# A decoder layer on one core: its first stage in a written order, and the inputs of later blocks staged ahead

## The chip, the core and the metric

The kernel runs on one core of a Trainium2 chip, written in Tile, a layer over the engines' instructions that places buffers, semaphores and the order of work. TensorE (PE; its weight loads are shown as PEld) multiplies matrices into PSUM banks, VectorE (DVE), ScalarE (ACT) and GpSimd (POOL) do elementwise work, SyncE (SP) issues most of the DMAs. The metric is the device time of one execution in microseconds.

## The reference, cut to what matters

One layer of a decoder over 2048 tokens of width 1024, all in float32:

```python
mod = jax.nn.silu(c) @ w_ada[l] + b_ada[l]
shift_a, scale_a, gate_a, shift_m, scale_m, gate_m = [
    m[:, None, :] for m in jnp.split(mod, N_MOD, axis=-1)]
h = rms_norm(x, g_attn[l]) * (1.0 + scale_a) + shift_a
proj = h @ w_in[l]
q_f, k_f, v_f, q_s, k_s, v_s, f_logit = jnp.split(proj, offsets, axis=-1)
o_fox = forgetting_attention(...)      # 8 heads, causal
o_sb = stick_breaking_attention(...)   # 8 heads, causal
x = x + gate_a * (mix @ w_out[l])
h = rms_norm(x, g_mlp[l]) * (1.0 + scale_m) + shift_m
u = causal_depthwise_conv(h @ w_up[l], conv_w[l], conv_b[l])
x = x + gate_m * ((jax.nn.silu(u_gate) * u_val) @ w_down[l])
return rms_norm(x, g_final)
```

The first work is the condition: `silu(c) @ w_ada` for the first two of six parts (shift and scale of the mixer), a vector of 2048 numbers from a matrix of 8.4 MB. No query, key or value can be computed before it.

## The kernel before, in words

**Precision.** A float32 matrix is split into a high half, rounded to the type that TensorE takes, and the remainder. `split` (L43) writes the high half with ScalarE (L44) and the remainder, the low half, with GpSimd or, where it is given, VectorE (L45). A product is three matmuls: high by high, high by low, low by high (`accumulate`, L323).

**Blocks and units.** The tokens are four blocks of 512 (`TB`). A unit is one kind of head, one pair of heads and one block. Units run in the order stick-breaking pairs 0 to 3, then forgetting pairs 0 to 3, each over its four blocks. The first four units (pair 0, "direct") are special: their blocks must first be read from x, normalized, transposed and modulated to h. h is then stored in DRAM (`hs`), and the other pairs read it back (`proj`, L446). The first block is `first_block` (L458), the next three are `norm_proj` (L495).

**The first stage.** c is transposed to a column and put through SiLU. `begin_block` (L180) loads the x of a block as four tiles of 128 x 1024 and normalizes them: a sum of squares on ScalarE (L95), its root (L96), a reciprocal and a scaling on VectorE (L104). `load_ada` (L190) loads w_ada in four groups, and `load_raw` (L209) the first pair's weights between them. `first_block` transposes x on PE and copies it to a stage in SBUF, by ScalarE and VectorE in turn. For each second of the eight 128-row tiles `mod_cols` (L253) makes four columns of shift and scale: ScalarE scales three of eight terms by the condition's column (L256), GpSimd adds them (L258), VectorE multiplies and adds the other five (L261), and PE sums over the partitions by a product with ones (L264). Then ScalarE applies scale and shift (L476), the result is split, and PE adds it to the query and the key sums. `finish_proj` (L350) evicts both in halves (L355, L356 for the query), copies them by DMA into the layouts that attention reads (L360, L375), and makes the values (L396), 24 matmuls for each 128 tokens.

**Differences of values.** Stick-breaking attention uses each value less the one before it. `steps_of_values` (L432) stores the values to DRAM (`vd`), reads them back one row later and subtracts on GpSimd (L441).

**Blocks 1 to 3.** `norm_proj` calls `modulate` (L106): for each tile four transposes into PSUM, scale and shift on VectorE (L114), a split, the store of h and the query product. Then comes `begin_block` of the next block, and `finish_proj`.

**What sets the order.** Attention is a generator of steps, and so are the projections. `interleave` and `pace` (L760) let a count of projection steps pass for each attention step; `proj_steps` (L731) says how many steps a unit has. What is written so is only a priority. At the end Tile simulates all instructions and issues on each engine, whenever it is free in that simulation, the earliest one in the program whose inputs and buffers are ready. Each engine, and SyncE's DMA queue, then runs its list strictly in that order on the chip. `tc.issue_after(ins)` adds the rule that what is traced in its block comes behind `ins` on `ins`'s engine. The kernel before uses it for the stores of the first block's h, three behind the key copies and five behind the fetch of the values (L487 to L493).

**Buffers that matter.** `xt` has four tiles of x; tags K and V have five tiles each, one for each block's keys and values and one to spare; `pt` has three PSUM banks, `pj` and `qk` two each.

## Time and profile before

| | |
|---|---|
| median of three runs | 3090.65 us (3089.12 to 3095.47) |
| profiled execution | 3093.19 us |
| its span, first to last instruction | 3091.5 us |
| mean granted TensorE clock | 0.986 |
| instructions in the profile | 45281 |

The profile is of one execution. A row of a group gives the line, the engine, the operation, the tiles it writes and reads, shapes, count, then the time it was busy in all, the mean of one in ns, and the idle time of the engine just before with what ended it. A row of the timeline gives start, length, engine, and in brackets the idle time before it. A row of the chain of waits gives start, length and what the chain that ended last did then. A granted clock of 0.50 means that TensorE ran at half speed.

### The profile page before, as it was taken

What the parts mean: (1) busy time and instruction counts of PE and PEld (TensorE: products, weight loads), DVE (VectorE), ACT (ScalarE), POOL (GpSimd) and SP (SyncE); (2) the same over time, 40 slices, a digit from 0 to 9 for tenths busy, and PEclk for the clock granted to TensorE, in tenths of its full rate; (3) what the DMA queues carried; (4) which work ended last, traced back from release to release, by engine and by line L of the source; (5) the groups of instructions that cost most, each with busy time, mean ns of one, the idle gap of its engine ahead of it and who ended that gap; (6) DMA issues with size and microseconds to landing.
All of it is one profiled execution on the core that took longest, in us unless ns stands there. A gap on an engine that the chain in (4) does not pass through costs nothing.

```text
span 3091.5 us, 45281 instructions
## 1 busy us (share of the span) xinstructions
PE 2944.7 (95%) x15902; PEld 2501.1 (81%) x15902; DVE 2079.9 (67%) x3174; ACT 1680.7 (54%) x3121; POOL 986.4 (32%) x1015
## 2 busy tenths in 40 slices
PE   6899999999999999999999899999899998999998
PEld 5788889888888898888877688888688887888887
DVE  5778778877876567578633677778977776254253
ACT  5667767777775656568643544444444444343332
POOL 4431222142122322321122344444444442332321
PEclk9999999999999999999999999999999999999999
DMA  7748756766479755856166522222322224555562
GB/s 236 264 139 305 235 192 204 285 230 216 166 239 348 248 186 183 295 196 222 59 214 224 183 82 85 85 83 80 92 75 82 82 82 158 179 198 170 180 204 86
DMA packets 302676, 546.79 MB, mean 177 GB/s; under 512 B 30992, under 2 KB 179216, under 8 KB 301424
## 3 DMA queue, kind: packets, MB, share of 16 engines
q1 hardware_dynamic: 289712, 531.24, 52.5%
q10 hardware_dynamic: 12736, 12.66, 1.2%
q8 instruction: 125, 2.05, 0.3%
q14 instruction: 103, 0.84, 0.1%
HBM read 407.14 MB, written 130.36 MB: 174 GB/s over the span
## 4 chain that ended last, share of the span: by engine, by line
PE 54%; DMA 13%; DVE 12%; POOL 8%; issue 8%; ACT 4%; SPq 1%; POOLq 0%; ACTq 0%; DVEq 0%
PE ps_pj L325 9%; PE ps_o L1155 8%; PE ps_pv L531 7%; PE ps_pt L522 6%; PE ps_pj L396 4%; PE ps_t L1155 4%; PE ps_o L1005 4%; PE ps_bc L1155 4%; DMA wuraw<-in_w_up_dram 3%; PE ps_qk L512 3%; PE ps_qk L513 3%; DVE wu L45 3%; DMA r<-rstd 2%; DVE u L1074 2%; POOL ws L993 2%
## 5 line engine op out<-in xcount | busy, mean ns | idle before, releaser
L1005 PE MATMUL ps_o<-oa,wu 128*128 128x512 f32 x2088 | 503.1, 392 | 14.5 <-DVE oa L45 7.0
L1005 PEld LDWEIGHTS ps_o<-oa,wu 128*128 128x128 f32 x2088 | 390.0, 188 | 106.0 <-DVE oa L45 11.6
L325 PE MATMUL ps_pj<-hp,w_qk 128*128 128x512 f32 x1512 | 420.7, 406 | 23.0 <-DMA hp<-hs 12.9
L527 DVE TENSOR_TENSOR at<-ps_pt,at 128x512 fp32r<-128x512 f32 (+1 forms) x576 | 366.3, 652 | 103.2 <-ACT at L526 100.0
L531 PE MATMUL ps_pv<-at,V 128*128 128x256 f32 x2304 | 407.8, 294 | 19.3 <-ACT at L526 7.6
L550 DVE TENSOR_TENSOR_SCAN a<-r,a 128x512 f32<-128x512 f32 (+2 forms) x320 | 370.1, 1175 | 79.4 <-ACT a L545 38.9
L526 ACT ACTIVATE at<-ps_pt 128x512 fp32r<-128x512 f32 (+1 forms) x576 | 318.7, 576 | 152.3 <-PE ps_pt L522 113.8
L531 PEld LDWEIGHTS ps_pv<-at,V 128*128 128x128 f32 x2304 | 336.3, 191 | 56.0 <-DVE at L527 19.7
L325 PEld LDWEIGHTS ps_pj<-hp,w_qk 128*128 128x128 f32 x1512 | 275.0, 192 | 78.3 <-DMA hp<-hs 15.0
L45 DVE TENSOR_TENSOR wd<-wdraw,wd 128x1024 fp32r<-128x1024 f32 x88 | 113.3, 1288 | 261.2 <-ACT wd L44 261.0
L512 PE MATMUL ps_qk<-K,Q 128*128 128x512 f32 (+2 forms) x640 | 264.8, 415 | 5.7 <-DVE mn L588 2.6
L1155 PE MATMUL ps_o<-wd,g 128*128 128x512 f32 x1040 | 250.4, 390 | 8.7 <-ACT g L44 8.7
L45 POOL TENSOR_TENSOR g<-graw,g 128x512 fp32r<-128x512 f32 x84 | 141.8, 1690 | 325.9 <-ACT g L44 316.8
L1005 PE MATMUL ps_t<-ob,wu 128*128 128x512 f32 x984 | 243.2, 392 | 0.0
L396 PE MATMUL ps_pj<-w_v,hp 128*128 128x256 f32 (+1 forms) x1536 | 237.4, 289 | 2.4 <-DVE q L356 1.0
L1155 PEld LDWEIGHTS ps_o<-wd,g 128*128 128x128 f32 x1040 | 195.9, 189 | 49.9 <-ACT g L44 9.2
L513 PE MATMUL ps_qk<-K,Q 128*128 128x512 f32 (+2 forms) x640 | 236.3, 370 | 0.0
L44 ACT ACTIVATE wu<-wuraw 128x512 fp32r<-128x512 f32 x214 | 133.2, 626 | 187.6 <-PE ps_o L1005 118.4
L396 PEld LDWEIGHTS ps_pj<-w_v,hp 128*128 128x128 f32 x1536 | 210.9, 190 | 13.4 <-DVE q L356 2.2
L1005 PEld LDWEIGHTS ps_t<-ob,wu 128*128 128x128 f32 x984 | 186.3, 189 | 39.1 <-ACT hf_m L910 0.2
L44 ACT ACTIVATE wd<-wdraw 128x1024 fp32r<-128x1024 f32 x88 | 93.0, 1057 | 212.6 <-PE ps_bc L1155 200.6
L544 ACT ACTIVATE r<-ps_qk 128x512 f32<-128x512 f32 (+2 forms) x320 | 173.2, 541 | 52.0 <-PE ps_qk L513 49.9
(226 smaller groups left out, 5480.6 us busy)
## 6 DMA issues: line engine op xcount, KB each, us to landing
hp<-hs SPq DMA_DIRECT2D x224, 512.0 KB
wuraw<-in_w_up_dram SPq DMA_DIRECT2D x84, 512.0 KB
wdraw<-in_w_down_dram SPq DMA_DIRECT2D x84, 512.0 KB
g<-u SPq DMA_DIRECT2D x42, 512.0 KB
graw<-g SPq DMA_DIRECT2D x84, 256.0 KB
hs<-hp SPq DMA_DIRECT2D x32, 512.0 KB
hp<-in_w_ada_dram SPq DMA_DIRECT2D x32, 512.0 KB
qk_fox<-q SPq DMA_DIRECT2D x32, 512.0 KB
```

What stands on the lines that cost most here:

```text
L44: nc.scalar.activation(hi, src, AF.Copy)
L45: (lo_engine or nc.gpsimd).tensor_sub(lo, src, f(hi))
L325: nc.tensor.matmul(acc, w[kt][:, a, n], h[:, bb], start=kt == 0 and i == 0, stop=kt == KT - 1 and i == 2)
L396: nc.tensor.matmul(av[:, t * width:(t + 1) * width], hts[kt][:, a, tok], w[1][kt][:, bb, 0:width], start=kt == 0 and m == 0, stop=kt == KT ...
L512: nc.tensor.matmul(b[:, :cw], Q[:, hl, 0, qcols], K[:, hl, :cw], start=True, stop=False)
L513: marks.append(nc.tensor.matmul(b[:, :cw], Q[:, hl, 1, qcols], K[:, hl, :cw], start=False, stop=True).ins)
L526: nc.scalar.activation(at[:, 0, lo:], b[:, lo:], AF.Copy)
L527: nc.vector.tensor_sub(at[:, 1, lo:], b[:, lo:], f(at[:, 0, lo:]))
L531: nc.tensor.matmul(o[:, 0:2 * P], V[kt // 4][:, kt % 4, hl, :], rhs, start=first and kk == 0 and w == 0, stop=last and kk == 1 and w == 1)
L550: nc.vector.tensor_tensor_scan(rev, r[:, 0:need][:, ::-1], rev, 0.0 if right[qi] is None else right[qi][:, 0:1], ALU.mult, ALU.add)
L1005: nc.tensor.matmul(b, w[:, p, j], o[:, q], start=first and i == 0, stop=last and i == 2, skip_group_check=True)
L1155: nc.tensor.matmul(banks[t][n], g[:, a, t * P:(t + 1) * P], w[:, b, n * TB:(n + 1) * TB], start=k == 0 and i == 0, stop=k == NKD - 1 and i ...
```

## The change

The first stage is written in a fixed order: every part is traced inside `fixed()`, which puts its instructions behind the last one so traced on each engine. The small loads move from ScalarE's queue to SyncE's, between and behind the large ones. The eight terms of a column are six on VectorE (the first a scaling), and two that go straight to PE as products with the condition's column (a constant moving operand); a reduction on VectorE adds the three sums. All stage copies are on ScalarE. The low halves of the first pair's weights and of h are on VectorE. Small products without a use (`keep_warm`) run before and between. The first block's h is stored tile by tile as it is made. x of block 1 is loaded in the first stage, normalized after the first pair's value weights, and transposed and modulated into free K buffers between the first four steps of `finish_proj` and its rest. Blocks 2 and 3 are staged in free K and V buffers as the first eight steps of their projection; then x of the next block is loaded, then come eight steps of split and product, then the normalization of the next block, then `finish_proj`. Scale and shift of staged tiles alternate between ScalarE and VectorE.

```diff
+    @contextmanager
+    def fixed():
+        with ExitStack() as order:
+            for ins in last.values():
+                order.enter_context(tc.issue_after(ins))
+            n = len(nc.cur_bb.bb.instructions)
+            yield
+        for ins in nc.cur_bb.bb.instructions[n:]:
+            last[ins.engine] = ins
...
+    begin_block(0)
     for r, src in ((R_GA, g_attn), (R_GM, g_mlp), (R_GF, g_out_fox), (R_GS, g_out_sb), (R_BA, b_ada)):
         n = src.shape[1] // P
-        nc.scalar.dma_start(rows[r:r + n], src[0].rearrange("(t p) -> t p", p=P))
...
+        nc.sync.dma_start(rows[r:r + n], src[0].rearrange("(t p) -> t p", p=P))
...
+    nc.sync.dma_start(wfr, w_in[:, 6 * 512:6 * 512 + NH].rearrange("(k p) n -> p k n", p=P))
+    begin_block(1)
+    for t in range(4):
+        nc.sync.dma_start(bf_c[t * NH:(t + 1) * NH], b_fgate.rearrange("o n -> n o"))
...
+    WARM = (8, 3)
+    DIRECT, FILL = 6, 1
+    SPLIT = 4
+    class mod_cols:
...
+        def add(self, k0, k1):
+            if k0 == 0:
+                self.t = px.tile([P, 2, 2 * P], F32, name="adas", tag="z", bufs=2)
+                nc.vector.tensor_scalar_mul(self.t, self.w[0], cs[:, 0:1])
+            for k in range(max(1, k0), k1):
+                nc.vector.scalar_tensor_tensor(self.t, self.w[k], cs[:, k:k + 1], self.t, ALU.mult, ALU.add)
+        def total(self, *ks):
+            for k in ks:
+                a, v = (self.t, ones[:, 0:1]) if k is None else (self.w[k], cs[:, k:k + 1])
+                b = self.b[:, 4 * len(self.terms):][:, 0:4]
+                self.terms.append(k)
+                for i in range(4):
+                    nc.tensor.matmul(b[:, i:i + 1], a[:, i // 2, i % 2 * P:(i % 2 + 1) * P], v, start=True, stop=True)
...
-            split(w[:, 0], w[:, 1], raw)
+            lo = nc.vector if (kind, p) == ("sb", 0) else None
+            split(w[:, 0], w[:, 1], raw, lo)
...
+    def keep_warm(n):
+        for _ in range(n):
+            nc.tensor.matmul(warm[:, 0:2 * P], ones, edge[:, 0:2 * P], start=True, stop=True)
...
+        def stage_h(kt):
+            hf = px.tile([P, TB], F32, name="hf_a", bufs=2)
             nc.scalar.activation(hf, stage[kt // 2][:, kt % 2], AF.Identity, scale=mod_a[:, 0, kt:kt + 1],
                                  bias=mod_a[:, 1, kt:kt + 1])
             h = h_tile()
             split(h[:, 0], h[:, 1], hf, nc.vector)
+            nc.sync.dma_start(hs[0][kt], f(h))
+            hts.append(h)
...
+        for g in range(KT // 2):
+            m = ms[g + 1]
+            if m:
+                do(m.add, 0, 3)
+            do(ms[g].finish)
+            if m:
+                total(m, *range(DIRECT, KT - 1))
+            do(stage_h, 2 * g)
+            do(project_h, 2 * g)
+            if m:
+                do(m.add, 3, DIRECT)
+            do(stage_h, 2 * g + 1)
+            if m:
+                do(w[1], 2 * g + 2)
+                do(w[1], 2 * g + 3)
+                total(m, None, KT - 1)
+            do(project_h, 2 * g + 1)
+        with fixed():
+            w[1:] = [w[2]()]
+        with fixed():
+            normalize_block(blocks[1])
+        g = finish_proj("sb", 0, 0, aq, w, hts, ak)
+        for _ in range(SPLIT):
+            next(g)
+        drain(stage_block(1))
+        drain(g)
+    def stage_block(tb):
+        xts = blocks[tb]
+        stages[tb] = []
+        for kt in range(KT):
+            if kt % 2 == 0:
+                t = sb.tile([P, 2, TB], F32, name="xm", tag="K" if kt // 2 < 5 - tb else "V", bufs=5)
+            b = pt()
+            for i, xt in enumerate(xts):
+                nc.tensor.transpose(b[:, i * P:(i + 1) * P], xt[:, kt * P:(kt + 1) * P], ident)
+            scale, bias = mod_a[:, 0, kt:kt + 1], mod_a[:, 1, kt:kt + 1]
+            if kt % 2:
+                nc.vector.tensor_scalar(t[:, 1], b, scale, bias, ALU.mult, ALU.add)
+            else:
+                nc.scalar.activation(t[:, 0], b, AF.Identity, scale=scale, bias=bias)
+            stages[tb].append(t[:, kt % 2])
+            yield
+    def norm_proj(tb, w):
+        if tb > 1:
+            yield from stage_block(tb)
+        else:
+            for _ in range(KT):
+                yield
+        if tb + 1 < NTB:
+            begin_block(tb + 1)
+        aq = pj()
+        hts = []
+        for kt in range(KT):
+            h = h_tile()
+            split(h[:, 0], h[:, 1], stages[tb][kt], nc.vector if kt % 2 else None)
+            nc.sync.dma_start(hs[tb][kt], f(h))
+            hts.append(h)
             accumulate(aq, 0, w[0], h, kt)
+            yield
         if tb + 1 < NTB:
+            normalize_block(blocks[tb + 1])
         yield from finish_proj("sb", 0, tb, aq, w, hts)
...
-            return 0 if tb == 0 else KT + 17
+            return 0 if tb == 0 else 2 * KT + 15
```

More of the change, by code (lines that the diff above doesn't have):

```diff
@@ new lines, with __init__, finish @@
+    warm = pj()
+    WARM = (8, 3)
+    DIRECT, FILL = 6, 1
+    SPLIT = 4
+    class mod_cols:
+        def __init__(self, g):
+            self.g = g
+            self.w = [adas[4 * g + k // 2][:, k % 2] for k in range(KT)]
+            self.terms = []
+            self.b = pt()
+        def add(self, k0, k1):
[11 more added lines that the diff above has]
+                    nc.tensor.matmul(b[:, i:i + 1], a[:, i // 2, i % 2 * P:(i % 2 + 1) * P], v, start=True, stop=True)
+        def finish(self):
+            g, n = self.g, len(self.terms)
+            k2 = slice(2 * g, 2 * g + 2)
+            m = sm.tile([P, 4], F32, name="msum", bufs=2)
+            nc.vector.tensor_reduce(m, self.b[:, 0:4 * n].rearrange("p (j i) -> p i j", i=4),
+                                    mybir.AxisListType.X, ALU.add)
+            nc.vector.tensor_add(mod_a[:, 1, k2], m[:, 0:2], cols[:, R_BA + 2 * g:R_BA + 2 * g + 2])
+            nc.vector.tensor_mul(m[:, 2:4], m[:, 2:4], cols[:, R_GA + 2 * g:R_GA + 2 * g + 2])
+            nc.vector.tensor_add(mod_a[:, 0, k2], m[:, 2:4], gba[:, k2])
```

138 lines of the change are left out of this document (47 added, 91 removed).

## The prediction

> **What bounds the kernel now.** I read the page first, then windows over the first 400 us, then the timeline, the groups of instructions and the chain of waits of the first 130 us. The page says which engine the whole leans on:
>
> ```profile
> span 3091.5 us, 45281 instructions
> PE 2944.7 (95%) x15902; PEld 2501.1 (81%) x15902; DVE 2079.9 (67%) x3174; ACT 1680.7 (54%) x3121; POOL 986.4 (32%) x1015
> ```
>
> TensorE (PE) is idle for 147 us in all. The windows show where (length, busy time of each engine with its count, granted PE clock, DMA share, GB/s):
>
> ```profile
> 0.00:28.00 28.00, 5.70 (x21) 3.87 (x22) 12.05 (x22) 14.96 (x31) 11.56 (x16) 1.00 0.98 303
> 28.00:47.00 19.00, 16.76 (x65) 12.85 (x65) 16.74 (x26) 12.50 (x29) 11.00 (x11) 1.00 1.06 350
> 47.00:60.68 13.68, 10.81 (x37) 8.83 (x36) 9.01 (x17) 10.90 (x22) 7.97 (x13) 0.50 0.02 5
> 74.30:88.00 13.70, 10.39 (x64) 8.32 (x62) 8.58 (x14) 7.37 (x20) 6.01 (x8) 1.00 0.76 281
> 88.00:94.80 6.80, 3.68 (x9) 2.91 (x10) 5.86 (x6) 3.38 (x6) 6.80 (x6) 0.50 1.03 420
> 94.80:160.00 65.20, 59.11 (x385) 51.13 (x384) 48.44 (x70) 43.40 (x91) 19.97 (x20) 1.00 0.74 247
> 160.00:240.00 80.00, 73.07 (x501) 64.88 (x500) 65.07 (x92) 52.32 (x114) 29.98 (x28) 0.99 0.46 149
> 240.00:400.00 160.00, 158.56 (x986) 139.35 (x986) 124.66 (x169) 114.46 (x252) 31.35 (x53) 1.00 0.81 272
> ```
>
> The change touches only work that ends before about 240 us. Up to there PE idles some 47 us, and the clock is halved in two stretches; from 240 on it is 99% busy. So a lead won before 240 us should reach the end: nothing after it waits for a clock on the wall.
>
> What delays the first block? In the groups of the first 75 us (busy us, mean ns | idle before), VectorE and GpSimd share the sums that make the modulation columns:
>
> ```profile
> L261 DVE SCALAR_TENSOR_TENSOR adas<-ada,cs,adas 128x512 f32<-128x512 f32 x16 | 16.9, 1054 | 0.2
> L266 DVE TENSOR_TENSOR mod_a<-ps_pv,cols 128x2 f32<-128x2 f32 x4 | 0.6, 156 | 3.9 <-PE ps_pv L264 3.9
> L104 DVE TENSOR_SCALAR xt<-xt,ss_a 128x1024 f32<-128x1024 f32 x8 | 7.5, 966 | 0.1
> L95 ACT ACTIVATE at<-xt 128x1024 f32<-128x1024 f32 x8 | 8.3, 1043 | 7.9 <-DMA bf_c<-in_b_fgate_dram 7.9
> L476 ACT ACTIVATE hf_a<-xT,mod_a 128x512 f32<-128x512 f32 x8 | 6.1, 806 | 9.5 <-DVE mod_a L269 9.5
> L468 ACT ACTIVATE xT<-ps_pt 128x512 f32<-128x512 f32 x4 | 2.2, 584 | 2.7 <-PE ps_pt L464 2.7
> L44 ACT ACTIVATE w_v<-raws 128x256 fp32r<-128x256 f32 x8 | 3.2, 403 | 0.0
> L258 POOL TENSOR_TENSOR ada<-ada 128x512 f32<-128x512 f32 x8 | 12.2, 1523 | 8.5 <-ACT ada L256 8.3
> ```
>
> The timeline shows the same addition at two prices, alone and while GpSimd works, and the end of the stage:
>
> ```profile
> 38.87 1.54 DVE L261 SCALAR_TENSOR_TENSOR adas<-ada,cs,adas 128x512 f32<-128x512 f32 x2
> 47.77 5.16 DVE L261 SCALAR_TENSOR_TENSOR adas<-ada,cs,adas 128x512 f32<-128x512 f32 x4
> 60.55 2.74 DVE L104 TENSOR_SCALAR xt<-xt,ss_a 128x1024 f32<-128x1024 f32 x4
> 64.16 0.60 ACT L355 ACTIVATE q<-ps_pj 128x512 fp32r<-128x512 f32 x1 [3.85 <-PE ps_pj L325]
> 65.17 0.68 DVE L356 SCALAR_TENSOR_TENSOR q<-ps_pj,q 128x512 fp32r<-128x512 f32 x1
> 65.27 1.17 SPq L375 DMA_DIRECT2D K<-q  x2
> 65.40 9.03 PE L396 MATMUL ps_pj<-w_v,hp 128*128 128x264 f32 x72 [0.68 <-DVE hp L405]
> 72.58 1.70 SPq L489 DMA_DIRECT2D hs<-hp  x3
> 74.34 0.36 PE L512 MATMUL ps_qk<-K,Q 128*128 128x256 f32 x1
> ```
>
> 0.77 us alone, 1.29 us beside the weight splits on GpSimd. Query and key sums are complete at 64.2 us, the value products at 74.4, and the first score starts at 74.34, when the copies of K and Q have landed. The chain then goes through a store and a load:
>
> ```profile
> 74.99 6.16 DMA vd<-hp
> 81.17 4.32 DMA hp<-vd
> 88.90 2.17 POOL hp L45
> 91.12 4.27 PE ps_pj L325 x10
> 95.39 0.44 PE ps_pt L112 x4
> 97.09 2.31 PE ps_pj L325 x10
> 114.15 1.28 ACT L96
> 116.01 2.73 DVE xt L104 x4
> 119.50 3.00 DMA vd<-hp
> 143.42 4.75 DMA xt<-in_x_dram
> ```
>
> GpSimd waits for the values to come back, and the low halves of block 1 stand behind it, so PE gets its next products at 91.1. Ten products take 4.27 us at half clock and 2.31 at full, four transposes 0.44.
>
> **The change part by part.** Is the DMA in the way? The loads, with their sizes, are
>
> ```profile
> ada<-in_w_ada_dram SPq DMA_DIRECT2D x32, 256.0 KB
> xt<-in_x_dram SPq DMA_DIRECT2D x8, 512.0 KB
> raws<-in_w_in_dram SPq DMA_DIRECT2D x16, 128.0 KB
> ```
>
> x, all of w_ada and half of raws are 2.1 + 8.4 + 1.05 = 11.5 MB. 28 us at 303 GB/s bring 8.5 MB, the other 3.0 take 8.7 us at 350: w_ada is in at 36.7 us. Raws' other half and x of block 1 are 3.1 MB more, in at 45.7. VectorE did the last sum at 52.9, so it was late, not the load.
>
> *Small loads move from ScalarE's queue to SyncE's.* Ten issues leave ScalarE, whose first square waited 7.9 us for them (L95's row). It can begin when the first quarter of x lands, at about 5.5 (an estimate: 2.1 MB at 303 GB/s take 7 us from the first issues at 1.3): four squares and roots with one table load, 4 x 1.33 + 1.28 = 6.6, and the scale, end near 14. SyncE issues ten more, but its loads are paced by the DMA anyway; cover: 46 us of full DMA.
>
> *Constant products.* Out go 12 scalings on ScalarE and 8 additions on GpSimd (12.2 us). VectorE now has six terms for each of four groups; terms 6 and 7 become products on PE with the condition column as the moving side. The low halves of the 16 weight tiles go from GpSimd to VectorE too. GpSimd is then empty, so I take 0.74 to 0.77 an addition. The first term is a scaling: at most 0.74 (an addition of its shape), at least 0.34 (half of the 0.69 that a scaling of twice its width takes, 2.74 for four); I take 0.42, nearest to that, as it is the same operation. A weight's low half has no row on VectorE: between 0.34 (half of the 0.68 at L356) and 0.68; I take 0.41. A reduction of 12 columns joins three small operations; four of L266's 0.16.
>
> *Fixed order.* VectorE's round for one group of two tiles is in line: 0.42 + 5 x 0.76 for the sums, 0.82 for two weights, 1.36 for two low halves of h, 0.64 for the small ones, and a wait of 1.5 while ScalarE does the shift (0.81) and the high half (0.60, as at L355): 8.5 us. From 14.4: first sums to 18.5; weights to 20.4, held by ScalarE's eight copies (8 x 0.58); three terms of the next group, 22.5; finish, 23.0. Three more rounds give 48.5, less 1.9 as no group follows, plus 1.4 for PE's last totals; shift and high half twice, 2.6; low half 0.7; six products at 0.23, 1.4. Queries and keys are complete at **53**, not 64.2: 11 us. The warming and filling products and 96 half-products of one column on PE cost nothing there: PE has 8.5 us a round and 12 products of 0.23 to do. If that cover went, 32 half-products more at 0.11 would add about 1 us after the last sum.
>
> *What takes it back.* Behind the last high half, ScalarE's fixed order has the value weights (8 x 0.40, with a small one in the shadow of each, 3.3) and the squares of block 1 (4 x 1.04, their reads and the root, 4.9). Query eviction is not in the fixed order, but comes later in the program, so the planner takes the ready squares first: 50.6 + 3.3 + 4.9 = 58.8, query high half to 59.4. VectorE scales four tiles (2.74 and a reciprocal) to 62.1, then two low halves: 63.5. The copies took from 65.27 to 74.34, 9 us; the last ones now land at about 72.3. Late next is thus the eviction, and who waits is SyncE's copies and unit 0's scores. Between ends: eviction first, scores at 64 to 66; squares held by a late x, beyond 74 (rivals). Nearest row: before, the squares ran in ScalarE's gaps ahead of the eviction.
>
> *PE meanwhile.* Of 96 value products at 0.125 us (the row of 72), 24 run from 53, 24 after the first copy-out, and 48 when VectorE is free at 62 to 63: 6 us, with 32 transposes of block 1 at 0.11 (3.5) between: 72.7. That is 1.7 earlier than 74.4 with 3.5 us of transposes done that the old kernel still had ahead: **-5.2**.
>
> *The h stores go out with each tile.* Eight of 512 KB move ahead of the copies. Each waits on SyncE for its low half; behind it stand the later stores, the copies and the next pair's weights, none of which is needed earlier. They queue behind the loads from 45.7, at 512 KB by 350 GB/s or 1.5 us each, and are gone by 58: cover, before the copies at 63. They no longer stand before the value store, which took 6.16 behind three of them and 3.00 in block 1: **-3.2**.
>
> *Later blocks.* x is loaded before the eight projection steps and scaled after them, in front of the value products, not behind them: the 1.28 + 2.73 us ahead of block 1's value store and the 4.75 for x in block 2 can go. Bounds: 0 (PE 91% busy there) to -8.8. I take -2.2, nearer to nothing, as PE does fill such waits. Modulation goes half to ScalarE (12 x 0.81 us more on it in 146 us, at 65% busy): beside PE's work. The half clock after 88 us costs 1.8 (3.7 us of products at half rate); with a shorter wait I take **-1**. Stages in K and V buffers: of five, one to three are held by units, the next unit is loaded after the last block is projected: nothing.
>
> Sum: -5.2 - 3.2 - 2.2 - 1.0 = -11.6 on the profiled execution, 3093.2 us (span 3091.5 and 1.7 around it): 3081.6. The median of the runs shown is 2.5 below that execution: **3079**.
>
> **The rivals.** *Eviction first.* If the simulated x of block 1 comes late, the planner puts the query eviction ahead of the squares; two high and two low halves end at 55.2, and the value products and transposes run through from 53 (12 + 3.5 us): PE has done them at 69, not 72.7, 3.7 us more: 3075. Against it: x was ready in the old order by then.
>
> *Clock.* The clock fell to 0.50 at 47, after a stretch in which PE was over three quarters busy, partly with one-column products. The same can hit the stretch of 57 to 63 here, where PE has 3 us of work: 9.6 us of products at half rate for 6.8 us cost 3.4, and the term of the clock (1.0) is gone: 3083. [...]
>
> *Nothing at the end.* The planner lays out blocks 1 to 3 anew; if the value store, the load and GpSimd's subtraction still decide in each block and other gaps open, the 11.6 us go there: 3090. For it: 13 us of idle PE from 94.8 to 240 in spite of its planning.
>
> *Slower.* If SyncE's order has the value weights and x of block 1 behind the h stores, they wait for the last split at 52: 3 + 6 us of loads after 53.5 end at 62.6, squares to 67.6, scaling to 70.8, copies at 81, 6.5 us later than before: 3097. It decides from where x lands after 57. Against it: the loads' buffers are free by 20 us, before the first h.
>
> **How the numbers follow.** Forecast 0.42, eviction first 0.18, clock 0.12, nothing 0.16, slower 0.12. Changes within 0.2% (6 us) can't be told from none. Faster: 0.60 of the first two, most of the clock's 0.12 and none of the rest, 0.69; same 0.18; slower 0.13. The forecast's own range, from the bounds of the later blocks and the first round, is 3072 to 3085; for 8 in 10 it must reach the nothing rival with some scatter and below the eviction-first one: 3066 (3075 less the other 6.6 us of the later blocks' bound, and a little) to 3094.
>
> **What would show it.** Queries and keys complete at 50 to 56 us; additions at 0.75 on VectorE; the value load landing near 80 instead of 85.5; the first score at 70 to 73. If ScalarE's query eviction stands before the squares, the first rival holds; if x of block 1 lands after 57, the last. Wrong altogether if PE's idle time before 240 us is not about 10 us smaller, or is and the rest of the span grows.

## The result, and the profile after

The changed kernel takes 3064.77 us (3060.69 to 3070.54, four runs) against 3089.89 us for the kernel before beside it: a ratio of 0.9912, with a 95% interval of 0.9896 to 0.9929. It is faster by 25 us; 11.6 were forecast, and the range ended at 3066. Two later sets of runs gave 0.9914 and 0.9911.

The page and the windows of the changed kernel, in the columns of those shown of before:

```profile
span 3059.0 us, 45489 instructions
PE 2950.6 (96%) x16012; PEld 2515.7 (82%) x16012; DVE 2085.6 (68%) x3190; ACT 1687.9 (55%) x3125; POOL 969.1 (32%) x983
...
0.00:28.00 28.00, 20.57 (x98) 17.82 (x99) 15.46 (x36) 16.69 (x31) 0.70 (x6) 0.87 0.93 295
28.00:47.00 19.00, 19.00 (x89) 16.61 (x88) 11.86 (x27) 6.79 (x12) 0.00 (x0) 0.74 0.94 274
47.00:60.68 13.68, 12.15 (x74) 9.99 (x73) 9.12 (x31) 9.59 (x28) 0.00 (x0) 1.00 1.02 375
88.00:94.80 6.80, 5.19 (x34) 4.30 (x33) 5.44 (x8) 5.95 (x13) 3.31 (x3) 1.00 0.99 389
94.80:160.00 65.20, 62.40 (x439) 56.59 (x438) 49.69 (x80) 45.75 (x96) 19.81 (x20) 1.00 0.59 190
160.00:240.00 80.00, 74.99 (x493) 67.17 (x492) 64.46 (x79) 58.43 (x123) 31.10 (x29) 0.98 0.60 210
```

GpSimd does next to nothing in the first 60 us (0.70 us), as meant. From 94.8 to 240 TensorE idles 7.8 us instead of 13.0. The clock is no longer halved at 47 and at 88, but it is earlier: the first window's mean is 0.87, the second's 0.74. The timelines of ScalarE, VectorE, TensorE, SyncE and GpSimd, one after the other:

```profile
5.14 1.06 ACT L95 ACTIVATE at<-xt 128x1024 f32<-128x1024 f32 x1 [2.36 <-DMA xt<-in_x_dram]
57.03 1.05 ACT L95 ACTIVATE at<-xt 128x1024 f32<-128x1024 f32 x1
58.69 0.58 ACT L367 ACTIVATE q<-ps_pj 128x512 fp32r<-128x512 f32 x1
...
13.75 3.90 DVE L262 SCALAR_TENSOR_TENSOR adas<-ada,cs,adas 128x512 f32<-128x512 f32 x5
20.15 0.49 DVE L260 TENSOR_SCALAR adas<-ada,cs 128x512 f32<-128x512 f32 x1 [0.29 <-DMA ada<-in_w_ada_dram]
22.36 0.16 DVE L276 TENSOR_REDUCE msum<-ps_pt 128x4 f32<-128x12 f32 x1
34.27 0.17 DVE L276 TENSOR_REDUCE msum<-ps_pt 128x4 f32<-128x12 f32 x1 [3.50 <-PE ps_pt L270]
42.78 0.17 DVE L276 TENSOR_REDUCE msum<-ps_pt 128x4 f32<-128x12 f32 x1 [0.16 <-PE ps_pt L270]
50.36 0.17 DVE L276 TENSOR_REDUCE msum<-ps_pt 128x4 f32<-128x12 f32 x1 [1.20 <-PE ps_pt L270]
54.52 0.42 DVE L45 TENSOR_TENSOR w_v<-raws,w_v 128x256 fp32r<-128x256 f32 x1
...
24.72 1.84 PE L270 MATMUL ps_pt<-cs,ada 128*128 128x1 f32 x8 [2.66 <-DMA ada<-in_w_ada_dram]
55.36 0.62 PE L337 MATMUL ps_qk<-hp,w_qk 128*128 128x512 f32 x2
69.86 0.35 PE L591 MATMUL ps_qk<-K,Q 128*128 128x256 f32 x1
78.63 8.50 PE L337 MATMUL ps_pj<-hp,w_qk 128*128 128x512 f32 x36 [0.64 <-POOL hp L45]
...
70.54 0.38 SPq L446 DMA_DIRECT2D vd<-hp  x1
74.99 0.38 SPq L452 DMA_DIRECT2D hp<-vd  x1
...
76.66 5.32 POOL L45 TENSOR_TENSOR hp<-xm,hp 128x512 fp32r<-128x512 f32 x3
81.95 2.84 POOL L453 TENSOR_TENSOR hp<-hp 128x1024 f32<-128x1024 f32 x1
```

Queries and keys are complete at 56.0 (before: 64.2), the first score is at 69.86 (74.34). So the first stage came out much as the prediction laid it out, and the larger part of the surprise lies behind it. To see where, I take the products of attention weights and values (L531 before, L610 after), which are the same in the same order in both kernels, and subtract their times: the lead of a run over the profiled run of before. At 96 us of the kernel before the lead is 5.3 us, with 24 projection products and 11 transposes done beyond what the kernel before has done there; at 162 it is 20.2, with 23 value products and 6 score products fewer done; at 335 it is 16.6 with the same work done, at 1165 13.4, at 1292 34.3, at the end 32.5. Between 335 and the end nothing was edited. The experiments had to say what this second half is.

### The profile page after: what moved, and what is told of

The parts are those of the page before. It is cut to its first block, busy times and chain, and to the rows that moved or that the text cites. A ratio compares the mean times of both kernels' runs of the same rounds, so it can differ in the third digit from the quotient of the medians.

```text
span 3059.0 us, 45489 instructions
## 1 busy us (share of the span) xinstructions
PE 2950.6 (96%) x16012; PEld 2515.7 (82%) x16012; DVE 2085.6 (68%) x3190; ACT 1687.9 (55%) x3125; POOL 969.1 (32%) x983
## 4 chain that ended last, share of the span: by engine, by line
PE 35%; DVE 6%; DMA 5%; POOL 4%; issue 3%; ACT 2%; SPq 1%; ACTq 0%; POOLq 0%; DVEq 0%
PE ps_o L1084 10%; PE ps_o L1234 8%; PE ps_t L1234 4%; PE ps_t L1084 4%; PE ps_bc L1234 4%; DMA wuraw<-in_w_up_dram 2%; DMA r<-rstd 2%; DVE wu L45 2%; PE ps_pv L610 1%; PE ps_pt L601 1%; PE ps_o L895 1%; POOL ws L1072 1%; DVE u L1153 1%; POOL wuraw L1071 1%; PE ps_bc L895 1%
## 5 line engine op out<-in xcount | busy, mean ns | idle before, releaser
L1084 PE MATMUL ps_o<-oa,wu 128*128 128x512 f32 x2088 | 503.5, 392 | 11.8 <-DVE oa L45 6.0
L337 PE MATMUL ps_pj<-hp,w_qk 128*128 128x512 f32 x1512 | 410.8, 403 | 12.4 <-DMA hp<-hs 9.9
L629 DVE TENSOR_TENSOR_SCAN a<-r,a 128x512 f32<-128x512 f32 (+2 forms) x320 | 367.8, 1165 | 78.6 <-ACT a L624 40.2
L610 PE MATMUL ps_pv<-at,V 128*128 128x256 f32 x2304 | 402.3, 292 | 12.4 <-ACT at L605 4.4
L610 PEld LDWEIGHTS ps_pv<-at,V 128*128 128x128 f32 x2304 | 332.8, 190 | 45.1 <-DVE at L606 13.1
L337 PEld LDWEIGHTS ps_pj<-hp,w_qk 128*128 128x128 f32 x1512 | 275.9, 190 | 69.6 <-DMA hp<-hs 13.4
```

The source lines that it names most:

```text
L337: nc.tensor.matmul(acc, w[kt][:, a, n], h[:, bb], start=kt == 0 and i == 0, stop=kt == KT - 1 and i == 2)
L610: nc.tensor.matmul(o[:, 0:2 * P], V[kt // 4][:, kt % 4, hl, :], rhs, start=first and kk == 0 and w == 0, stop=last and kk == 1 and w == 1)
L629: nc.vector.tensor_tensor_scan(rev, r[:, 0:need][:, ::-1], rev, 0.0 if right[qi] is None else right[qi][:, 0:1], ALU.mult, ALU.add)
L1084: nc.tensor.matmul(b, w[:, p, j], o[:, q], start=first and i == 0, stop=last and i == 2, skip_group_check=True)
```

## The experiments

The table holds each kernel's ratio, then leads (minus is earlier than the first profile of before) at 335, 1165 and 1347 us, and the growth between the first and the last of them, where the number of TensorE's products between the two points is the same to within two. LATE 13 shifts other work, so the two kernels with it are left out of the last columns.

| kernel | ratio (95%) | 335 | 1165 | 1347 | growth |
|---|---|---|---|---|---|
| changed | 0.9912 (0.9896 to 0.9929) | -16.6 | -13.4 | -32.5 | -15.9 |
| changed, again | 0.9914 (0.9896 to 0.9932) | -16.2 | -5.2 | -24.0 | -7.8 |
| changed, third | 0.9911 (0.9896 to 0.9925) | -15.3 | -8.2 | -25.9 | -10.6 |
| before, again | 1.0005 (0.9995 to 1.0015) | +0.3 | +3.1 | +2.0 | +1.7 |
| first stage only | 1.0005 (0.9993 to 1.0016) | -7.0 | -8.7 | -12.0 | -5.0 |
| first stage only, again | 0.9998 (0.9988 to 1.0009) | -6.3 | -3.3 | -5.8 | +0.5 |
| staging only | 0.9981 (0.9965 to 0.9997) | -4.7 | +5.7 | -12.3 | -7.6 |
| no warming products | 0.9936 (0.9911 to 0.9960) | -17.6 | -2.7 | -19.1 | -1.5 |
| no fixed order | 0.9987 (0.9974 to 1.0000) | +5.2 | +12.4 | -9.2 | -14.4 |
| eviction first | 1.0037 (1.0024 to 1.0050) | +15.1 | +26.9 | +10.0 | -5.1 |
| before, more steps | 1.0045 (1.0030 to 1.0060) | +6.4 | +6.2 | +6.2 | -0.2 |
| before, LATE 13 | 1.0022 (1.0011 to 1.0034) | -1.5 | | | |
| changed, LATE 13 | 0.9946 (0.9931 to 0.9961) | -14.5 | | | |
| block 1 only | 0.9942 (0.9925 to 0.9958) | -12.2 | -12.2 | -14.0 | -1.8 |
| blocks 2 and 3 only | 0.9924 (0.9908 to 0.9940) | -11.8 | -1.7 | -22.0 | -10.2 |
| load late | 0.9892 (0.9875 to 0.9909) | -17.4 | -9.6 | -29.9 | -12.5 |
| load late, again | 0.9918 (0.9904 to 0.9931) | -20.1 | -11.0 | -30.5 | -10.4 |
| before + block 3 | 0.9959 (0.9942 to 0.9975) | +1.8 | +7.7 | -13.6 | -15.4 |
| changed - block 3 | 0.9952 (0.9938 to 0.9966) | -15.9 | -12.3 | -14.1 | +1.8 |

Runs of one kernel scatter by up to 10 us to either side of their median (the kernel before gave 3083.04 to 3100.89 in one set of 26), so one profile's lead at the end is not worth more than that. The lead at 335 is: it came back to within 1.5 us in the repeated profiles, except for the late load (2.7).

**The two halves of the change.** *First stage only*: blocks 1 to 3 are done as before.

```diff
-        for _ in range(SPLIT):
-            next(g)
-        drain(stage_block(1))
         drain(g)
...
+        yield from modulate(px, pt, blocks[tb], mod_a, lambda kt: h_tile(), done, "a", True)
         if tb + 1 < NTB:
             begin_block(tb + 1)
...
             normalize_block(blocks[tb + 1])
```

> The new first stage with the old blocks 1 to 3 (no transposing ahead, old order of load, normalization and modulation). Theory A, 'lead and plan': the change wins about 17 us by 240 us, of which the first stage alone gives 6 to 10 (first score at 70 instead of 74.3, value store no longer behind the h stores), and whatever the end differs from that comes from the new plan of the unchanged middle, so the lead between 240 us and the end moves by 5 us or more in either direction. Rival B, 'all early': the lead at 240 us is kept to the end within 3 us, so 3080 to 3084. Rival C, 'staging makes the middle faster': without staging the lead doesn't grow after 650 us, within 3 us, whatever it is at 240.

It is no faster than the kernel before, although its profile is 7.0 us ahead at 335, so rival B, that an early lead is kept, does not hold. *Staging only* puts the staged blocks behind the old first stage:

```diff
         begin_block(1)
+        normalize_block(blocks[1])
...
+        for _ in range(3):
+            next(g)
+        drain(stage_block(1))
         drain(g)
```

> The old first stage with blocks 1 to 3 staged ahead as in the change. Theory A: queries and keys complete at 64 us as before, lead at 240 us 5 to 10 us from the later blocks alone, and the end differs from it by a plan of its own, 5 us or more. Rival B: the lead at 240 is kept within 3 us, 3080 to 3085. Rival C: the lead grows by 8 us or more between 650 and 1300 us as it does in the changed kernel.

It gains 7 us; its first score is at 76.3, later than before. The two halves alone give 0 and 7 us, together 25: something works only with both, or the halves set off something apart from themselves. The column of growth already holds the hint (-7.6 against -5.0 and +0.5).

**The warming products.**

```diff
-    WARM = (8, 3)
-    DIRECT, FILL = 6, 1
+    WARM = (0, 0)
+    DIRECT, FILL = 6, 0
```

> The changed kernel without the 11 + 12 products that are there only to keep the clock up; all else is the same, and their results are used by nothing. If the clock matters (one theory): granted clock below 1.0 through most of the first 60 us, products at 0.43 us, queries and keys complete 3 to 6 us later than 55.5, and the end 3 us or more later. If it doesn't (the other, as the prediction had it): VectorE's rounds set the pace, queries and keys complete at 55 to 57, end within 3 us, apart from a new plan in the middle.

Without them the lead at 335 is 17.6, with them 15.3 to 16.6, and the first score is at 70.5 instead of 69.9. In the first 335 us they neither cost nor bring anything that shows: the clock is halved for some 17 us of the first 60 either way (the means of the three windows to 60.68 are 0.90, 0.86 and 0.77 without them, 0.87, 0.74 and 1.00 with them), and not for most of it, as one theory had it. The time is 20 us under the kernel before instead of 25; the intervals overlap (0.9911 to 0.9960).

**The order in which ScalarE works.** With `fixed()` made empty the planner orders the first stage itself:

```diff
     def fixed():
-        with ExitStack() as order:
-            for ins in last.values():
-                order.enter_context(tc.issue_after(ins))
-            n = len(nc.cur_bb.bb.instructions)
             yield
-        for ins in nc.cur_bb.bb.instructions[n:]:
-            last[ins.engine] = ins
```

> The changed kernel with the fixed order taken away: the planner places the first stage. If the order is what brings the first stage forward: queries and keys complete at 58 us or later and the lead at 240 us is 3 us or more smaller than the change's 17. If the gain is from the work itself (GpSimd emptied, ScalarE's queue cleared): queries and keys complete within 2 us of 55.5 and the lead at 240 us is 15 to 19.

*Eviction first* takes only the normalization of block 1 out of the fixed order and traces it behind the query eviction, which was to show what the squares ahead of the eviction cost:

```diff
-        with fixed():
-            normalize_block(blocks[1])
         g = finish_proj("sb", 0, 0, aq, w, hts, ak)
-        for _ in range(SPLIT):
+        next(g)
+        normalize_block(blocks[1])
+        for _ in range(SPLIT - 1):
             next(g)
```

> The changed kernel with block 1's normalization taken out of the fixed order and traced behind the first step of the projection's end, so that the query and key evictions come first in the program. By the prediction's own step (eviction behind the squares costs): both evictions done by 57 us, first score at 64 to 67 instead of 69.9, lead at 240 us 3 to 4 us larger. If the copies and the transposes of block 1 are late anyway: the first score moves, but the lead at 240 us stays within 2 us. The end moves with a new plan by up to 15 us either way (theory A).

ScalarE's timeline with no fixed order:

```profile
17.33 1.75 ACT L44 ACTIVATE w_qk<-raws 128x256 fp32r<-128x256 f32 x4 [8.65 <-DMA raws<-in_w_in_dram]
18.99 1.04 ACT L95 ACTIVATE at<-xt 128x1024 f32<-128x1024 f32 x1
25.18 1.32 ACT L44 ACTIVATE w_qk<-raws 128x256 fp32r<-128x256 f32 x3 [5.06 <-DMA raws<-in_w_in_dram]
74.25 0.60 ACT L362 ACTIVATE q<-ps_pj 128x512 fp32r<-128x512 f32 x1 [4.89 <-PE ps_pj L332]
```

and with the eviction first:

```profile
47.95 1.06 ACT L95 ACTIVATE at<-xt 128x1024 f32<-128x1024 f32 x1 [21.99 <-DMA xt<-in_x_dram]
83.24 0.58 ACT L367 ACTIVATE q<-ps_pj 128x512 fp32r<-128x512 f32 x1
```

The planner puts work into ScalarE's queue whose data, by its own clock, should be there, and on the chip is not. Without the order, weight splits stand ahead of the first square of block 0, which starts at 19.0 instead of 5.1. The first score is at 86.7, and at 236 us the kernel is 2.2 us behind the kernel before, so the order is what brings the first stage forward, as the first half of the expectation had it. With the block-1 squares free, they stand ahead of the second group's shift and hold the queue for 22 us until x lands; the first score is at 95.8 and the kernel is slower than before. The expectation was wrong: the trial shows nothing of the cost of the squares behind the eviction. It shows another way to lose time, which is akin to the slower rival but not the same: SyncE issues x of block 1 ahead of the h stores, at 44.0 us (44.2 in the changed kernel), and what comes too early is the square in ScalarE's queue. The fixed order is what keeps that out.

**Steps and pace.** The staged blocks count six projection steps more each, which moves the pace. *Before, more steps* gives the kernel before six empty steps a block:

```diff
-        yield
+        for _ in range(KT - 1):
+            yield
...
-            return 0 if tb == 0 else KT + 17
+            return 0 if tb == 0 else 2 * KT + 15
```

> The kernel before, with nothing added but six empty steps ahead of each of the projections of blocks 1 to 3, and the count of steps to match: no instruction is new, only the order in which blocks 1 to 3 and their attention are written. Theory D, 'two plans': the written order of everything after block 3 is the same in both kernels, but its plan falls into one of two forms, and the second is better by about 20 us between 1165 and 1290 us. If the empty steps are enough to tip it: an end 8 to 15 us lower with a lead near 0 at 340 us. If the plan stays in the first form: within 3 us of the kernel before at the end as well as at 340 us.

It loses 13 us, 6 of them by 335, which neither half of the expectation has, and gains nothing in the middle: the count of steps isn't the source. *LATE 13* starts the preparation of the late weights a unit later, which lays out the middle anew for both kernels:

```diff
-    LATE, PER = 12, 3
+    LATE, PER = 13, 3
```

> The kernel before with the late modulation started one unit later (LATE 13 instead of 12): the first 600 us are as before, the middle is planned anew. Theory D: the end moves by 5 us or more, with no early lead at all. If the middle doesn't depend on such placement: within 3 us.

> The changed kernel with the late modulation started one unit later. Theory D: the lead to 600 us stays at 16 to 20 us, the end is not tied to the change's 25 and lies anywhere from 10 to 30 us below the kernel before; against the kernel before with the same edit it is 12 to 22 us faster, the early lead alone. Rival C (staging itself makes the middle faster): 25 us or more faster than the kernel before with the same edit.

The kernel before loses 6.6 us by it. The two medians are 24.4 us apart, much as with LATE 12, and so between the two bands. If the second half were one lucky layout, a new layout should have taken it away. This one didn't; others were not tried.

**Which block.** *Block 1 only* and *blocks 2 and 3 only* choose per block between the staged and the old way, in the new first stage:

```diff
-            return norm_proj(tb, weights[kind, p])
+            return (norm_proj_new if tb == 1 else norm_proj_old)(tb, weights[kind, p])
```

> The changed kernel once more, nothing edited, for a second profile of it. If the gain between 1165 and 1290 us of the kernel before (17 us in the first profile, in code that is the same in both) belongs to the changed kernel's plan, this profile has it again, at least 10 us, and a lead of 16 to 18 us at 335. If it was scatter of that one execution, the lead stays between 14 and 22 us from 335 to the end, and the median lies 3 to 5 us above the first profile, 3063 to 3066.

> Only block 1 is transposed and modulated ahead; blocks 2 and 3 are modulated as before, with x loaded behind the modulation. The new first stage alone had a lead of 7.0 us at 335, the whole change 16.6. If the gain lies in the first stage's own gaps on TensorE (32 transposes done while TensorE waited, and x of block 2 loaded eight steps earlier), this kernel keeps most of it: 12 to 15 us at 335. If it lies in blocks 2 and 3, it has 7 to 10. In time, by the lead at 335 alone and a middle like that of the other kernels without staging (5 to 8 us lost): 3083 to 3092 either way; if the middle follows the first blocks, 3070 to 3078.

> The mirror image: block 1 is modulated as before, blocks 2 and 3 are staged ahead. If the gain lies in the first stage's gaps: a lead of 7 to 10 us at 335. If in blocks 2 and 3: 12 to 15. If the two parts only add up, the leads of this kernel and its mirror image less 7.0 each sum to 9.6.

Two things follow. At 335 the parts add up: over the 7.0 of the first stage alone, block 1 brings 5.2 and blocks 2 and 3 bring 4.8, and 7.0 + 5.2 + 4.8 = 17.0 against 16.6 for the whole. Behind 335 they don't: blocks 2 and 3 bring a growth of 10.2, block 1 only 1.8. All three profiles of the changed kernel have the jump from 1165 on (19 us in the first, 19 in the second, 18 in the third), so it is no scatter. One result doesn't fit the leads: *block 1 only* is 18.9 us under the kernel before (13 to 23 by its interval), where the first stage alone is level with it, though at 335 block 1 brings only 5.2. Behind 335 the first stage alone gives its lead back and this kernel doesn't; why was not looked into.

*Load late* loads x of blocks 2 and 3 behind the products, as before:

```diff
-        if tb + 1 < NTB:
-            begin_block(tb + 1)
         aq = pj()
...
         if tb + 1 < NTB:
+            begin_block(tb + 1)
             normalize_block(blocks[tb + 1])
```

> The changed kernel with x of blocks 2 and 3 loaded behind the eight steps of split and product, as before, not ahead of them; the staging itself is kept. If the earlier load is what the later blocks gain by (the prediction's later blocks, up to 4.75 us of waiting for x a block), the lead at 335 falls from 16.6 to 8 to 12 us. If it is the transposing ahead into free buffers, it stays at 14 to 17. The time: 3064 to 3070 if only the early blocks count and nothing falls, 3070 to 3078 if the load counts.

> The changed kernel with x of blocks 2 and 3 loaded behind the products, once more, beside the changed kernel on the same chip. If it is the better version of the two, it is 3 to 10 us under the changed kernel again; if that was scatter, the two are within 3 us of one another.

> The changed kernel beside the version with the late load: 23 to 28 us under the kernel before, with 700 products in the stretch of 1165 to 1292 us and a lead of 15 to 18 us at 335.

Nothing falls: leads of 17.4 and 20.1, and ratios on both sides of the changed kernel's. Beside it on the same chip the late load was 7.9 us faster in the first set and 2.6 us slower in the second, so the first looks like scatter. No other kernel here beats the changed one by more than the intervals. The earlier load is worth nothing that shows; the transposing and modulating ahead is what the early blocks gain by. TensorE's waits from 60 to 335 us of each profile agree (engine, line, what for: us in total, times, longest), of before, the first stage only, and the changed kernel:

```profile
PE ps_pj L325 <- POOL hp L45: 7.4, 4, 5.8
PE ps_pv L531 <- DVE at L527: 2.4, 5, 1.0
```

```profile
PE ps_pt L592 <- DVE at L597: 5.7, 3, 2.8
PE ps_pt L106 <- DVE hf_a L108: 2.8, 1, 2.8
```

```profile
PE ps_pt L559 <- DVE xm L562: 3.8, 3, 2.8
PE ps_qk L591 <- ACT a L624: 2.6, 4, 1.3
```

All such waits add up to 20.2 us before and 18.7 with the new first stage, where the wait for GpSimd's low halves gives way to waits for VectorE, for its part of the attention weights (L597) and for modulation (L108). They are 15.0 with block 1 staged, 16.5 with blocks 2 and 3, and 12.6 with all; the second profiles of the first stage and of the changed kernel have 21.8 and 13.6, so differences under 3 us say nothing. A block whose modulated tiles lie ready needs only its splits when its products are due.

**Block 3.** The last pair takes the staging of block 3 alone: added to the kernel before, with nothing else of the change but its six projection steps, and taken out of the changed kernel with them.

```diff
-            return norm_proj(tb, weights[kind, p])
+            return (norm_proj_new if tb == 3 else norm_proj_old)(tb, weights[kind, p])
```

In the second kernel the condition is `tb < 3`.

> The kernel before with block 3 alone staged ahead, nothing else. If the staging of block 3 is what puts the middle's work into another order, this kernel has the order of the changed one from unit 4 on: in the stretch from 1165 to 1292 us of the kernel before (756 products of TensorE there) it has about 700, it gains 6 to 12 us between 335 and 1347, and its time is 5 to 14 us under the kernel before, with the first 240 us unchanged to within 3. If the middle only follows from an earlier start, or is scatter, it has 756 products there, gains less than 3 us after 335 and lies within 5 us of the kernel before.

> The changed kernel with block 3 alone modulated as before. If block 3's staging decides the middle: 756 products in that stretch, a lead of 13 to 17 us at 335 that grows by at most 4 to 1347, and a time 14 to 19 us under the kernel before (the changed kernel: 25). If it does not: about 700 products, a growth of 8 to 16, and 22 to 27 us under.

Both came out as the theory of block 3 has it in their order and in the sign of the growth; in size they missed: the first gains 15.4 us between 335 and 1347 instead of 6 to 12, and the second is 12.9 us under the kernel before instead of 14 to 19. The windows from 335 to 1347 us and from 1165 to 1292 us of the kernel before, and the same stretches of the program in the others, first of before, then changed, then before with block 3, then changed without it:

```profile
1165.00:1292.00 127.00, 116.35 (x758) 103.49 (x757) 81.50 (x209) 81.70 (x161) 42.63 (x57) 0.97 0.69 224
335.00:1347.00 1012.00, 974.27 (x6382) 872.64 (x6382) 726.41 (x1300) 685.73 (x1437) 291.06 (x383) 0.99 0.71 236
```

```profile
1151.60:1257.70 106.10, 101.42 (x702) 92.19 (x701) 77.00 (x200) 73.84 (x143) 29.39 (x43) 0.97 0.62 198
318.40:1314.50 996.10, 970.11 (x6384) 870.03 (x6384) 723.65 (x1301) 688.10 (x1436) 290.58 (x382) 0.99 0.71 239
```

```profile
1172.70:1276.70 104.00, 100.50 (x701) 92.21 (x700) 77.31 (x202) 73.14 (x142) 28.57 (x42) 0.97 0.61 200
336.80:1333.40 996.60, 970.55 (x6384) 871.82 (x6384) 719.45 (x1301) 685.78 (x1436) 292.23 (x382) 0.99 0.71 238
```

```profile
1152.70:1277.90 125.20, 115.79 (x758) 103.35 (x757) 81.24 (x209) 81.48 (x160) 42.44 (x57) 0.97 0.68 220
319.10:1332.90 1013.80, 976.90 (x6382) 876.02 (x6381) 725.46 (x1300) 685.19 (x1436) 290.68 (x383) 0.98 0.71 236
```

The counts are the fingerprint. In the short stretch TensorE has 758 products where block 3 is modulated in place and 702 where it is staged: 56 products of later pairs, some 15 us of work, stand elsewhere, most of them earlier. So the short stretch alone flatters the staged kernels, and the loss ahead of it (leads at 1165) belongs to the same shift. The long stretch has the same work in all four, 6382 to 6384 products: 1012.0 and 1013.8 us without block 3's staging, 996.1 and 996.6 with it, TensorE idle 37.7 and 36.9 us against 26.0 and 26.0. Some 12 of the 16 us gained are idle time; the rest is shorter busy time of the same products. The idle time is spread over TensorE's waits there, for h of the later pairs, which is read back from DRAM, for VectorE's scans and for the attention weights' halves; of before and of changed:

```profile
PE ps_pj L325 <- DMA hp<-hs: 12.9, 6, 6.0
PE ps_pt L522 <- DVE a L550: 8.3, 11, 2.1
PE ps_pv L531 <- ACT at L526: 4.0, 3, 2.4
```

```profile
PE ps_pj L337 <- DMA hp<-hs: 9.3, 8, 3.8
PE ps_pt L601 <- DVE a L629: 5.4, 11, 1.2
PE ps_pv L610 <- ACT at L605: 2.2, 3, 1.3
```

Over all profiles, the lead of the eleven with block 3 staged grows by 10.1 us on the mean between 335 and 1347 (1.5 to 15.9), that of the six without by 0.5 (-1.8 to 5.0). The ranges overlap; the counts in the short stretch don't. In time, block 3 alone brings 13.9 us and all the rest of the change 12.9; together that is 26.8, and the changed kernel's three sets gave 25.1, 25.4 and 28.3. The other parts don't add up like this: staging all three blocks behind the old first stage brings 7 us, less than block 3 alone, and the first stage brings 0 by itself. What in the staging of block 3 makes the planner order the later pairs in the other way, and why block 2's staging doesn't, was not tried; the empty steps alone don't do it.

**The first stage again.**

> The kernel before, nothing edited, for a second profile of it and for the scatter: its time against itself is 1.000 within 0.0015, and the points of its program up to 335 us come within 1.5 us of the first profile, those at 1347 within 5. If they differ by more, the leads read from single profiles are worth that much less.

> The new first stage alone once more. Its first profile had a lead of 7 us at 335 and of 6 at the end, but was the fastest of its ten runs, and their median was level with the kernel before. If a lead won before 240 us reaches the end, the time is 5 to 9 us under the kernel before and the first median was off; if the rest gives it back, the time is within 3 us of the kernel before again and this profile, if it is a middling run, shows where between 335 us and the end.

The kernel before repeats its own early points to within 1.0 us up to 236 and 0.3 at 335, and drifts by up to 5.0 us behind. The first stage alone has its lead of 6.3 at 335 again, none at 865 (+1.6), 5.8 at 1347 and 1.1 at the end, with a median 1.1 us under the kernel before. So its 7 us don't arrive in full. Where they go isn't settled: the second profile loses its lead between 476 and 865 us and has it again at 1292, both lose some 5 us behind 1549, and drifts of 2 to 5 us come without any edit.

## Why the prediction was wrong, point by point

**The first stage: right in its prices, one round too short.** Prices were right to a few hundredths: additions 0.78 (five in 3.90; predicted 0.74 to 0.77), the first scaling 0.49 (0.42), a weight's low half 0.42 (0.41). The first square is at 5.1 (5.5), the first finish at 22.4 (22.5 to 23.0), and the third round takes 42.78 - 34.27 = 8.5 us, as worked out. Queries and keys are complete at 56.0, not 53. The difference is in the second round: 34.27 - 22.36 = 11.9 us. "Is the DMA in the way?" was answered by the last sum alone; in that round the products of the constant waited 2.66 us for w_ada (row of 24.72), TensorE idled, and the granted clock was 0.50 from 24.2 to 37.8. In the second profile it was halved only to 29.7 and the round took 9.9 us, so some 2 of the 3.4 us too many are the clock's (an estimate from these two). "PE has 8.5 us a round and 12 products of 0.23 to do" left the clock out: VectorE waited 3.50 us for TensorE (row of 34.27). That "the warming and filling products cost nothing" held, and they didn't keep the clock up either (halved for some 17 us of the first 60 with them and without).

**The eviction.** It was put behind all four squares, at 58.8; it ran at 58.69, but behind one square. That the times agree is chance: the value weights began 3 us later than worked out, and three squares fewer stood ahead. From the first copy to the first score it took 10.1 us (59.8 to 69.9; before 9.1), and the first score came at 69.9 instead of 72.3. It followed the value products without a wait; in the second profile, where the eviction ran 2.3 us earlier, it waited 2.4 us for the copies and came at 69.9 too. This was half of the eviction-first rival. The term of -5.2 can't be read off alone. At 96 us the lead was 5.3, 5.2 and 4.1 in the three profiles, and the further 24 projection products and 11 transposes are worth some 6.7 us at the prediction's 0.23 and 0.11 (an estimate). In equal work that makes 12.0, 11.9 and 10.8, where the terms up to there, -5.2, -3.2 and -1.0, add up to 9.4. The first stage alone has 6.8 and 6.5 there, with the products of the kernel before; staging block 1 brings the rest.

**The value store: too large, and no longer decisive.** Store to load took 74.99 - 70.54 = 4.45 us instead of 6.18: 1.7, not 3.2. In the second profile it took 7.32, with a lead of 16.2 at 335 all the same. It was no longer the wait that ends last: GpSimd made low halves of block 1 first and subtracted from 81.95, and TensorE began a run of 36 of block 1's products at 78.63, not at 91.1, after a wait of 0.64 us for a low half.

**The later blocks: a term that was too small.** "I take -2.2, nearer to nothing, as PE does fill such waits" was mis-sized, and named the wrong cause. Between 96 and 335 us the lead in equal work grew by 4.3 to 4.6 us in the three profiles (an estimate, by the same prices). The load of x has no part in it (late load); staging block 2 has, some 4 us (15.9 less 12.2).

**"So a lead won before 240 us should reach the end: nothing after it waits for a clock on the wall."** This is the step that failed by most, and in both directions. Busy at 99% from 240 to 400 isn't busy to the end: 37.7 us of idle time lay between 335 and 1347, and the planner can order that stretch anew when the work ahead of it changes. Block 3's staging, whose buffers were costed at "nothing" and whose effect on the plan was not costed at all, changed the order of all later pairs and took 12 us of that idle time. In the other direction, the new first stage alone leads by 6 to 7 us at 335 and by nothing that shows in time. The prediction knew that the planner lays out blocks 1 to 3 anew, but only as the rival "nothing at the end", and only as a loss. Without block 3's staging the measured change is 12.9 us against the 11.6 of the forecast, though made of other parts.

**The rivals.** Slower: its sign, x of block 1 landing after 57, did not come, as SyncE issued that load ahead of the h stores; the squares of block 1 ran from 57.03 with no wait for x. What held two of the other kernels up was ScalarE's order. Clock: the granted clock was 1.00 from 47 to 94.8; the drop came earlier, at 24.2. The windows of the changed kernel around that stretch of half clock:

```profile
20.80:24.20 3.40, 1.26 (x9) 0.85 (x8) 1.98 (x6) 1.08 (x2) 0.00 (x0) 1.00 1.11 343
24.20:27.60 3.40, 2.88 (x11) 2.73 (x12) 2.94 (x5) 2.31 (x5) 0.00 (x0) 0.50 1.15 324
27.60:31.00 3.40, 3.40 (x13) 2.82 (x11) 3.10 (x6) 0.00 (x0) 0.00 (x0) 0.50 1.08 346
31.00:34.40 3.40, 3.40 (x15) 3.22 (x15) 0.13 (x1) 0.00 (x0) 0.00 (x0) 0.50 1.10 347
34.40:37.80 3.40, 3.40 (x10) 2.64 (x9) 1.79 (x6) 2.80 (x5) 0.00 (x0) 0.50 1.09 348
37.80:41.20 3.40, 3.40 (x25) 3.08 (x23) 3.29 (x7) 0.59 (x2) 0.00 (x0) 0.99 0.96 276
```

In the 3.40 us just ahead of this drop TensorE was busy for 1.26 us, and in the kernel before, in the 3.40 us ahead of the drop at 47, for 2.46. Behind the drop it was busy for 2.88 us of 3.40 and then throughout, as the records count busy time, and the clock stayed at 0.50 until 37.8. What makes the clock fall and come back was not shown.

## What to carry to other kernels

Where a planner orders the program, an edit has two prices: its own, and that of the order it gives to everything behind it; before a forecast says that nothing behind the edit changes, look for idle time there, because that is what a new order can win or lose. To tell the two apart, compare the times of the same instructions in both traces and the counts of instructions in a stretch: equal counts with a drift point to speed, unequal counts to another order. And do one part alone and all parts but one: here 13.9 and 12.9 us, of which only the second is near the forecast.

## What the runs showed of the hardware

In the changed kernel TensorE was busy in the records throughout from 27.6 to 37.8 us, at a granted clock of 0.50; in the 3.4 us from 37.8 on the clock was 0.99. About a third of that time (3.6 of 10.2 us) went to products with one column; what brings the clock back was not tried. In the first 100 us the kernel before had two stretches of half clock, 13.7 us from 47.0 and 6.8 us from 88.0, and the changed kernel two as well, 3.4 us from 13.9 and 13.6 us from 24.2. Runs of one and the same kernel differ by up to 10 us from their median, while the first 335 us of profiles of one kernel repeat to within 3 us (0.3 to 2.7 us at 335), so a cause that lies early can be read from single profiles and one that lies late can't.
